# Seven half products for eight in the large products of a transformer block

## The chip, the cores and the metric

The kernel runs on one core of one Trainium2 chip. The metric is the time of one launch on the device in microseconds (us), as the median of several runs. The core has a matrix engine (TensorE, PE in the profile), two engines for element-wise work (VectorE, DVE; GpSimd, POOL), one for activations (ScalarE, ACT) and one that issues transfers (SyncE, SP). Each has its own instruction stream and executes it in the order in which it is written. Matrix products land in PSUM, which PE, DVE and ACT reach; POOL works in SBUF alone.

## The reference

One block over 2048 latent tokens of 1024 channels, with 256 context tokens, all in float32:

```python
q, k, v, p, gt = split(modulate(x, sh1, sc1) @ w_in)         # 1024 | 256 | 256 | 512 | 2048 columns
attn_o = banded_attention(rope(q), rope(k), v, k_c, v_c, sink)  # +-128 tokens and all context keys
attn_d = attn_o @ w_attn_branch                              # 1024 x 1024
pool_d = (multiscale_pool(p) per group @ w_pool) * pool_scale
merged = sigmoid(gt[:, :1024]) * attn_d + sigmoid(gt[:, 1024:]) * pool_d
x = layernorm(ALPHA * x + g1 * (merged @ w_out), ln1_g, ln1_b)
u = layernorm(x) * (1 + sc2) + sh2
h = square(relu(u @ w_mlp_in))                               # 1024 x 4096
x = layernorm(ALPHA * x + g2 * (h @ w_mlp_out), ln2_g, ln2_b)   # 4096 x 1024
```

The modulation (sh, sc, g) is one vector for all tokens, a product of silu(c) with w_ada.

## The kernel before, in words

Every large product is made of float32r matmuls of a high and a low part. `split` (L52 to L57) casts an operand to its high part on ACT (L54) and subtracts to get the low part on DVE, or on POOL where that is asked for (L57). `mm3` (L59 to L63) makes three matmuls of a pair: high with high, high with low, low with high.

The first phase (up to L647) makes the projections to q, k, v and the attention, block by block of 128 tokens; it leaves the modulated, transposed input in `u_scr` and the attention output in `a_scr`, both in DRAM. Its last blocks run beside the channels of two pooling groups (`early_pool`, L572). The order of PE is written out there (`PLAN`, manual_schedule).

The second phase (from L649) runs over two chunks of 1024 tokens (L716). In each chunk all stages follow one another with their intermediate values in SBUF: pooling channels (`p_group`, `p_finish`), pooling gates and pooled maps (`pool_gate`), attention gates, attention branch and merge, output projection (`out_mm`) with the first normalisation (`ln_affine`, `ln1_u`) and the transposed input of the MLP (`u2_half`), then the MLP by groups of 256 hidden channels (`mlp_in`, `mlp_out`) with the second normalisation (`ln2`). Weights come in tiles of 1 MB through two raw buffers (`raw_tile`), are scaled by a gate vector on POOL where needed (L661) and split into two pairs of buffers (`wtile`, `wcols`). Sixteen steps of column sums over w_ada (`ada_load`, `ada_sum`) lie between the stages of the first chunk. `chan_mm` (L672 to L680) makes products with channels on the partitions. Here a scheduler orders each engine's instructions at compile time, PE's too, by the order of the program and by what is ready.

Tiles with one tag share a number of buffers: a new tile waits until the last reader of the one whose place it takes is done.

## Time and profile before

| | |
|---|---|
| median of 3 runs | 3173.37 us (3172.95 to 3176.61) |
| span of the profiled execution, its own time from first to last instruction | 3174.3 us |
| PE, PE's weight loads | 98%, 82% of the span |
| DVE, POOL, ACT | 56%, 36%, 36% |
| mean granted clock of PE | 0.993 |
| moved by transfers | 207 MB, mean 65 GB/s |

The profile is one execution. A busy time is the union of an engine's instructions; matmul records are pipelined and overlap, so the rate of PE is read from start to start. The granted clock is 1.00 at 2.4 GHz and 0.50 at 1.2 GHz. "A <- B" beside an idle time means that B ended last before A could start.

### The profile page before, as it was taken

Reading aid. Unit: us, or ns where it says so; the run is one execution under the profiler, and the core shown is the slowest. Engines: PE = TensorE matmul, PEld = TensorE weight load, DVE = VectorE, ACT = ScalarE, POOL = GpSimd, SP = SyncE. Lnnn points to the kernel's source line nnn. Section 1 sums busy time; section 2 is a strip of 40 time slices with the busy share of each in tenths; the row PEclk is TensorE's granted clock in tenths of the full one; section 3 lists DMA queues with packets and bytes.
Section 4 is the critical chain, followed back from the end, with each engine's and each line's share of the span. In section 5 each row is a group of like instructions: output and inputs, shape, how many; then the busy total and the mean of one; then the engine's idle time right before and its main releaser. Section 6 shows DMA issues by size and latency. Waiting matters only on the chain.

```text
span 3174.3 us, 41663 instructions
## 1 busy us (share of the span) xinstructions
PE 3096.2 (98%) x16104; PEld 2616.7 (82%) x16104; DVE 1780.8 (56%) x3136; ACT 1128.2 (36%) x1985; POOL 1151.8 (36%) x1419
## 2 busy tenths in 40 slices
PE   8899999998999999899999999999999999999998
PEld 5799899997988889788888888788898788888886
DVE  5678788887774446644444455821448444444446
ACT  4577777777621222521112112311214311121111
POOL 2877777776420052422122221410234321222123
PEclk9999999999999999999999999999999999999999
DMA  7111111113154430211111112411321111111111
GB/s 244 35 30 41 35 31 41 35 31 105 28 160 128 146 107 28 67 41 53 53 41 54 40 53 66 142 52 40 107 93 54 40 53 44 50 53 41 53 40 53
DMA packets 157846, 207.04 MB, mean 65 GB/s; under 512 B 7248, under 2 KB 132304, under 8 KB 157648
## 3 DMA queue, kind: packets, MB, share of 16 engines
q1 hardware_dynamic: 157648, 204.38, 20.5%
q8 instruction: 127, 2.08, 0.3%
q14 instruction: 71, 0.58, 0.1%
HBM read 179.19 MB, written 25.17 MB: 64 GB/s over the span
## 4 chain that ended last, share of the span: by engine, by line
PE 87%; DVE 7%; DMA 2%; issue 2%; POOL 1%; ACT 1%; SPq 0%; DVEq 0%; POOLq 0%; ACTq 0%
PE ps_y L62 7%; PE ps_y L63 7%; PE ps_y L61 7%; PE ps_h L677 7%; PE ps_h L680 7%; PE ps_h L678 7%; PE ps_o L497 4%; PE ps_pt L480 4%; PE ps_s L444 3%; PE ps_ga L677 2%; PE ps_ga L680 2%; PE ps_ga L678 2%; PE ps_ab L677 2%; PE ps_ab L678 2%; PE ps_ab L680 2%; PE ps_s L445 2%
## 5 line engine op out<-in xcount | busy, mean ns | idle before, releaser
L57 POOL TENSOR_TENSOR ht<-r,ht 128x512 fp32r<-128x512 f32 x128 | 172.0, 1346 | 1009.0 <-ACT ht L54 946.3
L974 DVE TENSOR_TENSOR acc<-ps_y,acc 128x512 f32<-128x512 f32 x464 | 314.7, 689 | 366.6 <-PE ps_y L63 366.5
L54 ACT CAST wh<-raw 128x2048 fp32r<-128x2048 f32 (+1 forms) x102 | 189.1, 1857 | 828.9 <-PE ps_y L63 471.6
L678 PE MATMUL ps_h<-u,wh 128*128 128x512 f32 x1024 | 406.2, 397 | 10.3 <-DVE u L57 10.3
L62 PE MATMUL ps_y<-wl,ht 128*128 128x512 f32 x1024 | 405.0, 396 | 1.7 <-DVE wl L57 1.7
L680 PE MATMUL ps_h<-u,wl 128*128 128x512 f32 x1024 | 404.7, 396 | 0.0
L63 PE MATMUL ps_y<-wh,ht 128*128 128x512 f32 x1024 | 403.2, 394 | 0.0
L677 PE MATMUL ps_h<-u,wh 128*128 128x512 f32 x1024 | 401.3, 398 | 0.0
L61 PE MATMUL ps_y<-wh,ht 128*128 128x512 f32 x1024 | 400.6, 393 | 0.0
L57 DVE TENSOR_TENSOR wl<-raw,wh 128x2048 fp32r<-128x2048 f32 (+1 forms) x100 | 228.1, 2282 | 202.8 <-ACT wh L54 202.8
L951 DVE TENSOR_TENSOR r<-r 128x512 f32<-128x512 f32 x128 | 142.7, 1119 | 300.6 <-ACT r L950 300.6
L57 DVE TENSOR_TENSOR pl<-ps_pt,ph 128x512 fp32r<-128x512 f32 x312 | 212.6, 686 | 70.4 <-ACT ph L54 68.4
L678 PEld LDWEIGHTS ps_h<-u,wh 128*128 128x128 f32 x1024 | 193.2, 189 | 57.0 <-DVE u L57 12.1
L459 POOL TENSOR_SCALAR s<-s,sm 128x640 f32<-128x640 f32 (+1 forms) x256 | 202.3, 798 | 99.1 <-DVE sm L458 53.7
L456 ACT ACTIVATE s<-s,sm 128x641 f32<-128x641 f32 (+1 forms) x256 | 210.2, 822 | 66.6 <-DVE sm L450 66.1
L62 PEld LDWEIGHTS ps_y<-wl,ht 128*128 128x128 f32 x1024 | 192.1, 188 | 47.6 <-DVE wl L57 2.3
L61 PEld LDWEIGHTS ps_y<-wh,ht 128*128 128x128 f32 x1024 | 192.3, 188 | 46.9 <-ACT r L950 0.3
L680 PEld LDWEIGHTS ps_h<-u,wl 128*128 128x128 f32 x1024 | 193.5, 189 | 45.4
L677 PEld LDWEIGHTS ps_h<-u,wh 128*128 128x128 f32 x1024 | 193.2, 189 | 45.1
L450 DVE CUSTOM_DVE_ANT_0 s<-ps_s,mask,nsink 128x640 f32<-128x640 f32 (+1 forms) x256 | 211.4, 863 | 31.2 <-PE ps_s L445 30.6
L63 PEld LDWEIGHTS ps_y<-wh,ht 128*128 128x128 f32 x1024 | 192.2, 188 | 44.4
L54 ACT CAST ph<-ps_pt 128x512 fp32r<-128x512 f32 x312 | 179.7, 581 | 110.7 <-PE ps_pt L480 107.6
(217 smaller groups left out, 6931.2 us busy)
## 6 DMA issues: line engine op xcount, KB each, us to landing
raw<-w_mlp_in SPq DMA_DIRECT2D x32, 1024.0 KB, 5.5
raw<-w_mlp_out SPq DMA_DIRECT2D x32, 1024.0 KB, 4.8
raw<-w_in SPq DMA_DIRECT2D x19, 1024.0 KB, 5.5
raw<-w_ada SPq DMA_DIRECT2D x16, 1024.0 KB, 5.2
raw<-u_scr SPq DMA_DIRECT2D x8, 1032.0 KB, 5.4
adaw<-w_ada SPq DMA_DIRECT2D x16, 512.0 KB, 8.1
xt<-x SPq DMA_DIRECT2D x16, 512.0 KB, 3.6
u_scr<-u SPq DMA_DIRECT2D x32, 256.0 KB, 3.1
```

What stands on the lines that cost most here:

```text
L54: act.copy(hi, src)
L57: (lo_eng or dve).tensor_tensor(lo, src, hi.bitcast(F32), ALU.subtract)
L61: pe.matmul(ps, sh, mh, start=first, stop=False)
L62: pe.matmul(ps, sh, ml, start=False, stop=False)
L63: pe.matmul(ps, sl, mh, start=False, stop=last)
L450: dve.tensor_tensor_reduce(out=s[:, 0:n], in0=pieces[z][2], in1=mk[z], op0=ALU.add, op1=ALU.min, scale=-1.0 / math.sqrt(HD), scalar=nsink[ ...
L456: act.activation(s[:, 0:n + 1], s[:, 0:n + 1], AF.Exp, bias=sm[:, 0, j:j + 1], scale=-1.0, accum_out=sm[:, 1, j:j + 1])
L459: pool.tensor_scalar(s[:, 0:n], s[:, 0:n], sm[:, 2, j:j + 1], 1.0, ALU.mult, ALU.mult)
L677: pe.matmul(ps, wh[:, k, c:c + P], mh, start=k == 0, stop=False)
L678: pe.matmul(ps, wh[:, k, c:c + P], ml, start=False, stop=False)
L680: pe.matmul(ps, wl[:, k, c:c + P], mh, start=False, stop=k == KT - 1)
L974: dve.tensor_tensor(a, ps, a, ALU.add)
```

## The change

The first phase stays as it is. Behind it the pooling channels and pooled maps of both chunks are made first, and the maps go to DRAM (`pd_scr`). Then come, each over all tokens, the attention branch, both gates and the merge, the output projection with the first normalisation, the first MLP product, and the second one; their results go to DRAM between the stages (`ab_scr`, `mg_scr`, `x1_scr`, `u2_scr`, `h_scr`, the last 32 MB in size).

Every product of a stage is cut into items: a contraction over 1024, with 1024 x 1024 values of one operand that are fixed for a stage (`Fill`: 1024 tokens, or 1024 rows of w_out or w_mlp_out) and 1024 x 256 values of the other that are streamed (`Stream`: 256 weight columns, or 256 tokens). Both are cut in two along both dimensions, and the four blocks of the result come from seven products of blocks in Winograd's form of Strassen's scheme: the sums of blocks are made in float32 ahead of the split into two parts (`Combos`), three products start a PSUM bank (numbers 1, 6, 5) and four are added into one of these banks after DVE or ACT has read it (2, 7, 4, 3).

There are 96 items: 8 of the attention branch, 16 of the gates, 8 of the output projection, 32 of each MLP product. The fixed operand changes 10 times. An item's 7 products have 4 x 3 matmuls of 128x128 with 512 columns each. The whole second phase now has PE's order written out (`ms2`); the other engines are still ordered by the scheduler.

```diff
+    ms2.enter_context(tc.manual_schedule(engines={mybir.EngineType.PE}))
+    def rtile(...):  tag="R", bufs=8        # parts of the streamed operand
+    def etile(...):  tag="ext", bufs=2      # two of the sums; also the copy xn and the pooled maps
+    def rwtile(...): tag="rw", bufs=3       # raw fixed operand; the fourth tile is a raw_tile (2, with the streams)
+    def ltile(p): 8 slots for products 1, 2; 8 for 6, 7; 12 for 5, 4, 3   # four per product
+    class Combos:
+        def add(self, eng=None):
...
+                e.tensor_tensor(v[0], b12, b11, sub)
+                e.tensor_tensor(v[1], b22, v[0], sub)
+                e.tensor_tensor(b12, b22, b12, sub)
+        def late(self, eng=None):
+            e.tensor_tensor(b11, b12 if self.kind == "A" else b21, self.v[1], ALU.subtract)
...
+    class Stream:                            # Combos on POOL
+        def step(self, p):
+            t = rtile([P, 2, 4, P])
+            split(t[:, 0], t[:, 1], self.c.src(p))
+            self.t[p] = t
+            if p == 1:
+                self.c.late()
...
+    class Fill:
+        def load(self):
+            for j in range(4):
+                raw = rwtile([P, 2, 2, 512]) if j < 3 else raw_tile([P, 2, 2, 512])
+                sp.dma_start(raw.rearrange("p k h n -> p k (h n)"), self.src(j))
+                if self.scale is not None:
...
+                        (pool if j % 2 else dve).tensor_tensor(v, v, g, ALU.mult)
...
+            for j in (0, 1):
+                self.c[j].add()
+        def step(self, p):
+            every = range(4)
+            if p == 1:
+                self.split(1, every)
+                self.c[0].late()
+                self.c[1].late()
+            elif p in (6, 7):
+                self.split(p, (0, 1))
+            elif p in (2, 4):
+                self.split(p, every)
+            elif p == 5:
+                self.split(5, (0, 1))
+                for j in (2, 3):
+                    self.c[j].add(dve)
+                    self.c[j].late(dve)
+                for q in (6, 7, 5):
+                    self.split(q, (2, 3))
+            else:
+                self.split(3, every)
+    def prod(ps, p, R, L, first):
+        r = R.t[p]
+        for k in range(4):
+            m = L.t[p, k]
+            mm = ((r[:, 0, k], m[:, 0]), (r[:, 0, k], m[:, 1]), (r[:, 1, k], m[:, 0]))
+            for i, (a, b) in enumerate(mm):
+                pe.matmul(ps, a, b, ...)
+    def run_items(items):                    # the loop's body, for item it with the next one nxt
+            if n + 2 < len(items):
+                items[n + 2].stream.load()
+            nfill = nxt.stage if nxt and nxt.stage is not it.stage else None
+            if nfill:
+                nfill.load()
...
+            if nxt:
+                nxt.stream.c.add()
+            def after(p):
+                if nfill:
+                    nfill.step(p)
+                if nxt:
+                    nxt.stream.step(p)
+            X = ps2("ps_x")
+            prod(X, 1, R, L, True)
+            x = sttile("cx")
+            act.copy(x, X)
+            it.sink("x", x)
+            after(1)
+            Y = ps2("ps_y")
+            prod(Y, 6, R, L, True)
+            u2_ = sttile("cu")
+            dve.tensor_tensor(u2_, Y, x, ALU.add)
+            it.sink("u2", u2_)
+            after(6)
+            prod(X, 2, R, L, False)
+            it.sink(11, X)
+            after(2)
+            prod(Y, 7, R, L, False)
+            u3_ = sttile("cv")
+            dve.tensor_tensor(u3_, Y, x, ALU.add)
+            it.sink("u3", u3_)
+            after(7)
+            Z = ps2("ps_z")
+            prod(Z, 5, R, L, True)
+            it.sink(22, u3_, Z)
+            after(5)
...
+            prod(Y, 4, R, L, False)
+            it.sink(21, x, Y)
+            after(4)
+            prod(Z, 3, R, L, False)
+            it.sink(12, u2_, Z)
+            after(3)
...
+    def acc_sink(i, scaled, last):           # output projection and second MLP product
+        def begin():
+            for b in range(2):
+                a = ldp[0].tile([P, D], F32, name="acc", tag="acc", bufs=2)
...
+                sp.dma_start(a, (x if last == "ln1" else x1_scr)[rows, :])
+                if scaled:
+                    act.mul(a, a, ALPHA)
...
+        def sink(key, t, z=None):
+            if key == "x":
+                pool.tensor_tensor(at(21), at(21), t, ALU.add)
...
+            else:
+                dve.tensor_tensor(at(key), t if key == 11 else z, at(key), ALU.add)
+                if key in (21, 12):
+                    ... last_of(...)         # normalise where it is the last sum, then store
+    def h_sink(c, n):                        # first MLP product
...
+                dve.tensor_tensor(o, z, t, ALU.add)
+                dve.scalar_tensor_tensor(o, o, 0.0, o, op0=ALU.max, op1=ALU.mult)
+            sp.dma_start(h_scr[:, 2 * n + h, t0:t0 + 512], o)
```

The sinks of the gates load the pooled map or the branch, apply the sigmoid on ACT, multiply on DVE, and for the pooling gate add the stored other half on POOL; each block of 128x512 is stored. Twelve steps of the column sums over w_ada now lie at the starts of items of the branch and the gates (four and eight items), four in the first MLP product. In the output projection each of the two token blocks of an item is normalised, stored, normalised a second time (`xn`), transposed on PE in the next item and stored modulated.

## Rows read from the trace of the kernel before

**Rows 1.** The page's first part: busy time, share of the span, instructions.

```profile
PE 3096.2 (98%) x16104; PEld 2616.7 (82%) x16104; DVE 1780.8 (56%) x3136; ACT 1128.2 (36%) x1985; POOL 1151.8 (36%) x1419
```

**Rows 2.** Timeline of PE in three stretches: start us, length us, instruction.

```profile
1601.10 0.40 PE L62 MATMUL ps_y<-wl,ht 128*128 128x512 f32 x1
...
1611.79 0.39 PE L63 MATMUL ps_y<-wh,ht 128*128 128x512 f32 x1
...
2400.55 0.29 PE L61 MATMUL ps_out<-wh,mg 128*128 128x256 f32 x1
...
2401.97 0.28 PE L61 MATMUL ps_out<-wh,mg 128*128 128x256 f32 x1
...
880.61 0.32 PE L677 MATMUL ps_p<-uh,wh 128*128 128x344 f32 x1
...
889.11 0.32 PE L677 MATMUL ps_p<-uh,wh 128*128 128x344 f32 x1
```

**Rows 3.** Tile ps_p: count, ns min/median/max, first to last start.

```profile
L677 PE MATMUL ps_p<-uh,wh x144: 313/320/422, 866.7 to 2105.9; 128*128 128x344 f32 x144
```

**Rows 4.** Timeline at the end of the launch.

```profile
3159.58 0.39 PE L63 MATMUL ps_y<-wh,ht 128*128 128x512 f32 x1
...
3170.50 0.99 SPq L995 DMA_DIRECT2D out<-acc  x2
```

**Rows 5.** Waits of PE behind the attention: us in total, times, longest.

```profile
PE ps_pd L61 <- ACT poh L54: 7.0, 1, 7.0
```

**Rows 6.** Tiles r, acc and raw, columns as in rows 3.

```profile
L951 DVE TENSOR_TENSOR r<-r x128: 679/693/3984, 1302.8 to 3119.3; 128x512 f32<-128x512 f32 x128
L54 ACT CAST ht<-r x128: 619/622/640, 1303.5 to 3120.0; 128x512 fp32r<-128x512 f32 x128
L57 POOL TENSOR_TENSOR ht<-r,ht x128: 1264/1293/3221, 1304.2 to 3120.7; 128x512 fp32r<-128x512 f32 x128
...
L974 DVE TENSOR_TENSOR acc<-ps_y,acc x464: 642/692/697, 1379.7 to 3164.6; 128x512 f32<-128x512 f32 x155
...
L698 DVE SCALAR_TENSOR_TENSOR adacc<-raw,cs,adacc x94: 475/485/2023, 899.9 to 1061.0; 128x256 f32<-128x256 f32 x94
L661 POOL TENSOR_TENSOR raw<-raw,gb x40: 4599/4628/6725, 1120.6 to 3080.1; 128x2048 f32<-128x2048 f32 x40
```

**Rows 7.** Timeline of DVE and POOL in two stretches.

```profile
1277.05 2.28 DVE L57 TENSOR_TENSOR wl<-raw,wh 128x2048 fp32r<-128x2048 f32 x1
1279.24 4.58 DVE L92 SCALAR_TENSOR_TENSOR mv<-mv 128x1 f32<-128x1 f32 x1
...
1277.15 6.65 POOL L661 TENSOR_TENSOR raw<-raw,gb 128x2048 f32<-128x2048 f32 x1 [2.10 <-DMA raw<-w_mlp_out]
...
2497.51 3.66 DVE L972 SCALAR_TENSOR_TENSOR acc<-acc,ps_y 128x512 f32<-128x512 f32 x6
...
2498.71 4.62 POOL L661 TENSOR_TENSOR raw<-raw,gb 128x2048 f32<-128x2048 f32 x1
```

**Rows 8.** Timeline of PE behind a wait, and stretches: us, busy (count), clock, DMA share, GB/s.

```profile
1275.92 1.22 PE L678 MATMUL ps_h<-u,wh 128*128 128x512 f32 x2 [4.78 <-DVE u L57]
...
1276.00:1278.00 2.00, 2.00 (x5) 1.63 (x6) 2.00 (x4) 2.00 (x5) 0.85 (x1) 0.50 0.22 88
1278.00:1280.00 2.00, 2.00 (x8) 1.60 (x8) 2.00 (x2) 0.53 (x2) 2.00 (x1) 0.76 0.00 0
```

**Rows 9.** Tile acc in the normalisations, columns as in rows 3.

```profile
L897 DVE SCALAR_TENSOR_TENSOR acc<-acc,mv,lnp x23: 737/757/2424, 1997.9 to 3160.5; 128x512 f32<-128x512 f32 x23
...
L898 POOL TENSOR_TENSOR acc<-acc,lnp x23: 1264/1303/3080, 2015.0 to 3165.0; 128x512 f32<-128x512 f32 x23
```

**Rows 10.** DMA issues: count, KB each, median us to landing.

```profile
raw<-w_mlp_out SPq DMA_DIRECT2D x32, 1024.0 KB, 4.8
...
acc<-x SPq DMA_DIRECT2D x16, 512.0 KB, 4.8
out<-acc SPq DMA_DIRECT2D x15, 512.0 KB, 2.6
```

More of the change, by code (lines that the diff above doesn't have):

```diff
@@ new lines, in prod, with __init__ @@
+    def prod(ps, p, R, L, first):
[4 more added lines that the diff above has]
+            for i, (a, b) in enumerate(mm):
+                pe.matmul(ps, a, b, start=first and k == 0 and i == 0, stop=k == 3 and i == 2, skip_group_check=not first)
+    class Item:
+        def __init__(self, stage, stream, sink, begin=None):
+            self.stage, self.stream, self.sink, self.begin = stage, stream, sink, begin
@@ L683, in block_kernel @@
-    ones = lp.tile([P, P], F32, name="ones")
+            uh, ul = uu[k]
+            for i, ps in enumerate(pss_):
+                pe.matmul(ps, wh[:, k], uh[:, UP[i]:UP[i] + 344], start=k == 0, stop=False)
+                pe.matmul(ps, wh[:, k], ul[:, UP[i]:UP[i] + 344], start=False, stop=False)
+            for i, ps in enumerate(pss_):
+                pe.matmul(ps, wl[:, k], uh[:, UP[i]:UP[i] + 344], start=False, stop=k == KT - 1)
+        pt = ptp.tile([P, PW], F32, name="pt1", tag="pt1", bufs=2)
@@ L684, in block_kernel, with w_fill, row, bias_row @@
+    def w_fill(src, scale=None):
+        v = src.rearrange("(k j p) n -> p j k n", k=2, j=4)
+        return Fill("B", lambda j: v[:, j], scale)
+    def row(name):
+        return stp.tile([P, D], F32, name=name, tag="row", bufs=2)
+    def bias_row(name, c0):
+        r = row(name)
+        sp.dma_start(r, b_row[c0:c0 + D].partition_broadcast(P))
+        return r
+    ones = stp.tile([P, P], F32, name="ones")
     dve.memset(ones, 1.0)
-    gb = [lp.tile([P, D], F32, name=f"gb{i}") for i in range(2)]
```

657 lines of the change are left out of this document (351 added, 306 removed).

## The prediction

> **What bounds the kernel now.** I read the page's engine table first: TensorE (PE) is busy 98% of the span [rows 1]. Matmul records overlap, so I counted starts. Beside each other, 128x512 matmuls of the MLP start 0.2324 us apart (1601.10 to 1611.79, 46 intervals), the 256-column ones of the output projection 0.118 us (2400.55 to 2401.97, 12 intervals), the 344-column ones of the pooling channels 0.157 us (880.61 to 889.11, 54 intervals) [rows 2]. The phase behind the attention starts on PE at 866.7 [rows 3] and its last matmul starts at 3159.58; the launch ends 14.7 us after that [rows 4]. Its matmuls are 8448 of 512 columns (MLP 6144, gates 1536, attention branch 768), 1536 of 256, 432 of 344 and 96 for the pooled maps: 1963 + 181 + 68 + 22 = 2234 us, with about 20 us of transposes and column sums (estimate, from their counts). From 866.7 that ends at 3121; the real end leaves some 39 us for all waits of PE, the longest one 7.0 us [rows 5]. So this phase is matmul-bound nearly everywhere, and fewer matmuls are time, if the other engines keep up.
>
> **What is removed.** Each large product becomes 96 items of 7 x 4 x 3 = 84 matmuls of 512 columns: 8064 x 0.2324 = 1874 us for the 2144 before, 270 us less; one item is 19.5 us. Pooling's 90 us and the 20 us stay. The floor is 866.7 + 1874 + 90 + 20 + 14.7 = 2865 us, on the profiled execution's 3174.3, which is 0.9 us above the runs' median, so I add nothing for that. Everything below is what hinders this floor.
>
> **What is added on the other engines.** The parts are split after the sums, so per item seven 128x512 parts of the streamed operand are cast on ACT (0.62 us each, 4.3 in all: no bound) and subtracted on DVE (0.69 us, D), and POOL makes four sums (1.29 us, G) [rows 6]. The question is whether D and G add up. The timeline says they do: at 1277.15 a POOL product that usually takes 4.63 us took 6.65, behind a 2.28 us DVE subtraction, and a DVE operation on one column then took 4.58 us, until POOL was done. DVE additions that read PSUM ran six in 3.66 us beside such a POOL product [rows 7]. The median and the maximum agree: 0.693 and 3.98 us with both inputs in SBUF, 0.692 and 0.697 us with one in PSUM [rows 6]. So I count D and G as one serial resource, "the port", and operations with a PSUM input outside it.
>
> The Trainium skill, "SBUF — State Buffer", "Who interferes with whom", states the same lock and that the loser waits for the whole instruction. Against a heavy price stands the median of that product with both inputs in SBUF, which is its undisturbed time: in this trace the two seldom meet. With no lock at all a hand-over below would cost 9 us, with the lock 17; I take the lock.
>
> Port time of an item: stream 7D + 4G = 10.0 us. The attention branch adds none; MLP in adds G + 3D: 13.4; MLP out adds 3G: 13.9; gates 4D, and 4G in each second item: 12.8 and 17.9, with 3.7 us of modulation sums (7 x 0.485 plus one) in eight of them, where a pair then averages 19.1 [rows 6]. All fit into 19.5 on average. With a normalisation it is more: per token block two POOL and two DVE operations (1.30 and 0.76 us [rows 9]) and small ones, about 4.1 us. MLP out with LN2: 13.9 + 8.2 + 1 = 23.1. The output projection has 3G, two blocks and a second statistic: 24.1.
>
> **Stalls, item by item.**
> - *Hand-overs, 10 of them.* The fixed operand's 28 parts fill exactly the 28 slots, so part p of the next stage can be written only after the last item's product p and is needed one item later: between the end of product 1 and the start of the next item's last product lie 33.5 us. Into them must go 28D for the parts, 8D of sums on DVE, 2G, twelve D and four G of the next stream, and some 5.8 us of sinks: 51.9 us less what can be put off. Lower bound 9 us over (the stream after next is postponed), upper 29 (nothing overlaps, and the fourth raw tile, which shares two buffers with the streams, comes a 4.8 us transfer late [rows 10]). I take 17, nearer the lower end because the order written down gives the fill precedence. Five of the hand-overs also scale their tile: 4 x 1.4 + 4 x 2.3 = 14.8 us of port, at best hidden in earlier items (0), at worst all of it; I take 4. Sum 170 + 20 = 190, bounds 90 to 364. These holes also cost clock: behind a wait of 4.78 us the granted clock was 0.50, the 1.2 GHz level, for two us and 0.76 on average for the next two [rows 8]. That is inside the 17.
> - *First fill and end of pooling.* The last pooled map (a chain of about 15 us) and the first 28 parts follow each other; PE order is fixed by hand there. 30 us (15 to 38), and 10 (0 to 25) for pooling's own chains; the 7.0 us wait of before [rows 5] is one of these.
> - *Output projection with LN1, 8 items.* Port alone 24.1 - 19.5 = 4.6 us over. There are also only two accumulator tiles: add, statistics and affine about 8 us, second statistics and copy about 5, reload 4.8, scaling and one POOL addition 2.6: 21 us from one use to the next. With DVE's PSUM reads and eight statistics counted as D each not hidden at all it is 33.7. I take 26.4: 55 us, bounds 37 to 114.
> - *MLP out with LN2, 8 items.* 3.6 to 10.5 us over; I take 4.4: 35 (29 to 84).
> - *Gates.* DVE's five PSUM reads (3.4 us) come to the 19.1: 0 to 3 us in eight items, so 0 to 24; I take 12.
> - *Accumulators elsewhere.* Store 2.6 and load 4.8 us [rows 10] end about 9 us into the next item; the PSUM bank waiting is used again two items later. Nothing; if that cover went, one product's wait, counted in the next point.
> - *In every item* PE waits twice for DVE to read a bank before it adds to it, with one product (2.8 us) between. DVE is in order, and one POOL operation in front of it eats 1.3 us of that. 0 to 1.3 us per item, I take 0.5: 45 us (0 to 125).
> - *SP's queue* gains stores and reloads: at most 5 MB in an item of gates. 1 MB lands in 4.8 us [rows 10], so that could fill it; I charge nothing beyond the upper bounds, since loads are two items ahead.
>
> Sum: 2865 + 190 + 30 + 10 + 55 + 35 + 12 + 45 = **3242 us**, taken as 3240, 2% slower. With all lower ends 3036, with all upper ends 3639.
>
> **Rivals.**
> - *Faster: the port is not felt.* POOL's sums fall where DVE reads PSUM or waits, and the order chosen for POOL, DVE and SP reaches ahead (loads, scaling and the first sums of a fill in the items before). Then DVE alone sets the hand-over: 36D + 12D + about 9 us of sinks is 42 in 33.5 us, 9 over, ten times 90; LN stages cost their lower ends 66, the start 25, handshakes 15: 2865 + 196 = 3061 us. For it: port use is below 14 of 19.5 us in 64 of 96 items, and the attention ran with long DVE and POOL times and few PE waits [rows 1, 5]. Against it: the 4.58 us row [rows 7], and that a fill is a dense run of just the operations that exclude each other. It decides once a hand-over costs under about 10 us. The Trainium skill, "Perfetto Trace Analysis", "Optimizing Scalar/DVE Operations", leans against this rival: moving work from DVE to GpSimd may not help, since they share a read port.
> - *Much slower: latency, not throughput.* Each sum waits in a chain (slot free, cast, subtract, two scratch tiles handed from the fill to the stream and back), engines execute in a fixed order, and PE at 1.2 GHz doubles each product that follows a hole. With hand-overs of 36 us, LN items of 33.7 and 1.3 us in each item: 2865 + 360 + 40 + 198 + 125 = 3588 us at its worst, about 3450 in the middle. For it: PE's two LN stretches show such chains already [rows 5, 8]; against: they lost only a few us there.
> - *The floor is reached.* All hidden but the start: about 2900 us. Against it: the LN stages exceed the item on the port alone.
> - *The change doesn't do what it says:* if sums were not fewer matmuls PE would stay at 3121 plus all stalls, near 3500. The count of 84 per item excludes it; I give it nothing.
>
> **How the numbers follow.** Forecast, 3180 to 3400: 0.48. Port not felt, 3000 to 3167: 0.31. Floor: 0.04. Much slower, over 3400: 0.13. Within 0.2% (6 us, about what a measurement can tell): 0.04. So faster 0.35, same 0.04, slower 0.61. The range takes the rival in, 3050 to 3450; the forecast's own is 3180 to 3400.
>
> **What would show it.** PE should hold 8064 + 528 large matmuls behind 866.7 at 0.232 us start to start inside an item, and items of 19.5 to 20.5 us in MLP in and out. Each change of the fixed operand should show a hole or a slow stretch of 15 to 25 us with DVE and POOL together near the whole window and DVE subtractions of 1.3 to 2 us; the LN items should take 24 to 28 us. The step on the port is wrong if DVE subtractions keep 0.69 us at the hand-overs; the step on hand-overs is wrong if PE's items there take under 29 us; the floor is wrong if plain items take over 21 us.

## The result, and the profile after

The changed kernel takes 3467.37 us (median of 4 runs, 3466.19 to 3470.29), beside 3174.85 us (3172.95 to 3176.61) for the kernel before: 1.092 times, 95% interval 1.091 to 1.094. Slower was forecast, but 3240 us; the time lies 17 us above the range of 3050 to 3450, and 67 us above the forecast's own, 3180 to 3400.

The page first. It gives each engine's busy time, and below that its busy tenths and TensorE's granted clock in 40 slices of the span; this is the changed kernel, to be held against [rows 1].

```profile
PE 2938.9 (85%) x14184; PEld 2432.6 (70%) x14184; DVE 2391.2 (69%) x3965; ACT 1556.1 (45%) x2867; POOL 1745.8 (50%) x1890
...
PE   8899999999858989797666599979996969789576
...
DVE  4687788877676787867555766685567575666775
...
PEclk9999999999879989898878799989997989899788
```

PE has fewer matmuls (14184, before 16104), but it is busy 85% of a longer span instead of 98%. Its row is full (9) only in stretches, and in every slice in which it falls to 7 or less the clock's row shows 8 or less. So the work went, as forecast, and more waiting came than work went.

To find the dents I use one regular mark of an item: ACT's copy of the first product (`cx`). ACT's timeline of the changed kernel (start, duration, engine, line, operation) around the change from the first to the second stage of the first MLP product:

```profile
2211.76 0.59 ACT L850 COPY cx<-ps_x 128x512 f32<-128x512 f32 x1 [2.17 <-PE ps_x L805]
...
2231.09 0.59 ACT L850 COPY cx<-ps_x 128x512 f32<-128x512 f32 x1 [2.17 <-PE ps_x L805]
...
2250.43 0.59 ACT L850 COPY cx<-ps_x 128x512 f32<-128x512 f32 x1
...
2291.64 0.57 ACT L850 COPY cx<-ps_x 128x512 f32<-128x512 f32 x1
...
2319.03 0.59 ACT L850 COPY cx<-ps_x 128x512 f32<-128x512 f32 x1 [2.13 <-PE ps_x L805]
```

Start to start, a plain item takes 19.3 us. The last item of a stage takes 41.2 here and the next stage's first one 27.4. Below, the price of a hand-over is what these two take above 2 x 19.3: here 30.0 us. The windows of the same kernel (busy times, then granted clock, DMA share, GB/s) show a plain stretch and this hand-over:

```profile
2020.00:2194.00 174.00, 174.00 (x757) 141.86 (x756) 110.71 (x163) 47.26 (x80) 61.69 (x45) 1.00 0.39 126
...
2250.40:2319.00 68.60, 45.03 (x169) 35.00 (x169) 59.80 (x69) 24.07 (x43) 31.07 (x18) 0.80 0.37 128
```

In the plain stretch PE never stops, at 174.00 / 757 = 0.230 us for a matmul, where the forecast took 0.2324 [rows 2]. In the hand-over DVE is busy 59.8 of 68.6 us, and PE, at a mean clock of 0.80, takes 45.03 / 169 = 0.266 us for each. The same windows over all ten hand-overs give 279 us of idle PE and 466 us of busy PE, where twenty items of 19.3 us are 386. So some 80 of the 359 us that they cost are not waits but slower matmuls around the waits, at mean granted clocks of 0.75 to 0.84 (a few of the 80 are transposes).

With all 96 marks the time adds up: the first product of the items starts at 994.7 instead of 956.7 (866.7 + 90); 96 items at 19.3; what they take beyond that; and the end of the launch as forecast. LN1 and LN2 are the two normalising stages, the output projection and the last MLP output stage; plain items are the 62 outside of these, the hand-overs and both ends.

| us above the floor | forecast | measured |
|---|---|---|
| start of the items | 10 | 38 |
| first item | 30 | 35 |
| ten hand-overs, with scaling | 190 | 359 |
| output projection with LN1 | 55, and a part of the floor's 20 for transposes and column sums | 130 in its six middle items (the rest is in two hand-overs) |
| last MLP stage with LN2 | 35 | 62 in six middle items |
| gates, handshakes in every item | 12 + 45 | 16 in 62 plain items |
| item of 84 matmuls | 19.5 | 19.3: 19 us less in all |

PE's waits behind 860 us, in the changed kernel (who waits for what: total, times, longest):

```profile
PE ps_x L805 <- ACT La L57: 151.7, 10, 17.9
PE ps_z L805 <- DVE acc L1110: 107.1, 21, 10.1
PE ps_u L1144 <- ACT xn L1138: 55.8, 6, 11.8
PE ps_y L805 <- DVE Lb L60: 41.5, 11, 5.1
```

The first row has one wait for each of the ten hand-overs (the first product needs a part of the fixed operand's fourth tile, which comes last); the second and the third lie mostly in the normalising stages. Before, PE's longest wait behind the attention was 7.0 us [rows 5]. The dearest hand-over is the one out of the output projection, 60.7 us; the other nine cost 23 to 45.

Who is slow in the hand-over is in DVE's groups of 2250.4 to 2319.0 by form (busy us, mean ns of one, then idle time before them):

```profile
L60 DVE TENSOR_TENSOR R<-raw,R 128x512 fp32r<-128x512 f32 x10 | 11.5, 1170 | 0.7 <-ACT R L57 0.7
L763 DVE TENSOR_TENSOR rw<-rw,gb 128x1024 f32<-128x1024 f32 x4 | 7.7, 1975 | 0.0
...
L60 DVE TENSOR_TENSOR Lc<-rw,Lc 128x512 fp32r<-128x512 f32 x6 | 3.8, 681 | 0.0
...
L1170 DVE SCALAR_TENSOR_TENSOR cv<-cv 128x512 f32<-128x512 f32 x2 | 3.6, 1778 | 0.0
```

Undisturbed, 512 columns take 0.68 us (third row), as [rows 6] said; beside POOL the same operations take 1.2 to 1.8. All of this trace behind 1000 us says so too. Of DVE's two-input operations (TENSOR_TENSOR) on 512 columns, 662 had both inputs in SBUF and no POOL operation beside them for over 0.1 us: at most 0.70 us each. 459 had both in SBUF and POOL beside them: 1.26 us on average, up to 2.88. 215 had an input in PSUM and POOL beside them: at most 0.69. And L763, which isn't this stage's, stands here: it scales the weights of the stage after, whose buffers have just come free.

### The profile page after: what moved, and what is told of

The parts are those of the page before. It is cut to its first block, busy times and chain, and to the rows that moved or that the text cites. A ratio compares the mean times of both kernels' runs of the same rounds, so it can differ in the third digit from the quotient of the medians.

```text
span 3464.2 us, 42248 instructions
## 1 busy us (share of the span) xinstructions
PE 2938.9 (85%) x14184; PEld 2432.6 (70%) x14184; DVE 2391.2 (69%) x3965; ACT 1556.1 (45%) x2867; POOL 1745.8 (50%) x1890
## 5 line engine op out<-in xcount | busy, mean ns | idle before, releaser
L805 PE MATMUL ps_x<-La,R 128*128 128x512 f32 x2304 | 601.5, 410 | 173.4 <-ACT La L57 151.7
L805 PE MATMUL ps_z<-Lc,R 128*128 128x512 f32 x2304 | 589.6, 407 | 107.2 <-DVE acc L1110 107.1
L805 PE MATMUL ps_y<-Lb,R 128*128 128x512 f32 x2304 | 596.0, 407 | 87.9 <-DVE Lb L60 41.5
L805 PEld LDWEIGHTS ps_x<-La,R 128*128 128x128 f32 x2304 | 452.0, 197 | 289.5 <-ACT La L57 156.1
L805 PEld LDWEIGHTS ps_z<-Lc,R 128*128 128x128 f32 x2304 | 452.5, 198 | 217.0 <-DVE acc L1110 98.3
L57 ACT CAST R<-raw 128x512 fp32r<-128x512 f32 (+1 forms) x486 | 301.1, 626 | 660.0 <-PE ps_z L805 310.0
L805 PEld LDWEIGHTS ps_y<-Lb,R 128*128 128x128 f32 x2304 | 447.2, 195 | 209.0 <-DVE Lb L60 45.9
L60 DVE TENSOR_TENSOR R<-raw,R 128x512 fp32r<-128x512 f32 (+1 forms) x486 | 452.0, 934 | 109.3 <-ACT R L57 107.2
L805 PE MATMUL ps_y<-Lc,R 128*128 128x512 f32 x1152 | 294.2, 406 | 6.6 <-DVE cv L864 6.4
L805 PEld LDWEIGHTS ps_y<-Lc,R 128*128 128x128 f32 x1152 | 224.6, 197 | 56.4 <-DVE cv L864 8.8
L453 DVE CUSTOM_DVE_ANT_0 s<-ps_s,mask,nsink 128x640 f32<-128x640 f32 (+1 forms) x256 | 211.3, 862 | 29.6 <-PE ps_s L448 29.4
```

The source lines that it names most:

```text
L57: act.copy(hi, src)
L60: (lo_eng or dve).tensor_tensor(lo, src, hi.bitcast(F32), ALU.subtract)
L453: dve.tensor_tensor_reduce(out=s[:, 0:n], in0=pieces[z][2], in1=mk[z], op0=ALU.add, op1=ALU.min, scale=-1.0 / math.sqrt(HD), scalar=nsink[ ...
L805: pe.matmul(ps, a, b, start=first and k == 0 and i == 0, stop=k == 3 and i == 2, skip_group_check=not first)
```

## The experiments

I call **excess** what DVE's operations of 512 and 1024 columns take above 0.68 and 1.36 us each, added up from the by-form groups of the two items of all ten hand-overs. It measures how long DVE stood behind POOL: 141 us in the changed kernel. (Undisturbed, 1024 columns take 1.21 us, so the sum is some 3 us too small where there are 20 of them.) The letters L, P, Q and so on are the theories that each expectation names. A time without a range is that of one run. Edits are to the changed kernel unless a base is named. Base "swap and table" is e1 with e2; it did not run by itself, and its 3368 us and hand-over sum of about 307 are added up from the two.

**e1: the late fourth tile.** Its buffer is shared with the streams, whose load was issued first.

```diff
-            if n + 2 < len(items):
-                items[n + 2].stream.load()
             nfill = nxt.stage if nxt and nxt.stage is not it.stage else None
             if nfill:
                 nfill.load()
+            if n + 2 < len(items):
+                items[n + 2].stream.load()
```

> The changed kernel with one edit: at a hand-over the next fixed operand is loaded before the stream tile of the item after next, so its fourth raw tile takes the raw buffer that is free at the start of the last item and not the one that the next item's splits hold until its end. Theory L (the hand-over is a latency: the fourth raw tile lands late and its seven parts hold PE): the hole of some 15 us before the first product of a new stage goes, the ten hand-overs fall from 338 us over the plain items to about 170, total near 3300 us. Theory P (the hand-over is the throughput of DVE and POOL on their shared port): the same work has to be done, the hand-overs stay at 300 to 340 us, total 3430 to 3470 us.

3403.5 us, hand-over sum 312: the tile was late, but this is worth 46 us in the hand-overs, not the 168 of theory L. Theory P had the sum right and the time too long. In the hand-over shown above 30.0 turned only into 29.1. The 15 us hole ahead of the first product went, and other waits took its place (PE, 2224.6 to 2292.3):

```profile
PE ps_y L805 <- ACT Lb L57: 8.3, 1, 8.3
PE ps_y L805 <- DVE cv L864: 6.9, 1, 6.9
PE ps_y L805 <- DVE cu L856: 2.9, 2, 2.1
```

DVE's timeline in e1 says why `cv` comes late:

```profile
2265.88 0.68 DVE L856 TENSOR_TENSOR cu<-ps_y,cx 128x512 f32<-128x512 f32 x1
2266.48 1.15 DVE L60 TENSOR_TENSOR R<-raw,R 128x512 fp32r<-128x512 f32 x1
2267.56 6.74 DVE L763 TENSOR_TENSOR rw<-rw,gb 128x1024 f32<-128x1024 f32 x2
2274.22 1.52 DVE L60 TENSOR_TENSOR R<-raw,R 128x512 fp32r<-128x512 f32 x1
2275.67 4.48 DVE L763 TENSOR_TENSOR rw<-rw,gb 128x1024 f32<-128x1024 f32 x2
```

Between `cu` and `cv`, both of which PE waits for, the next stage's scaling holds DVE for over 11 us; four such operations undisturbed are 4.8 (1.21 each).

**e2: activation tables.** In the output projection ACT's timeline of the changed kernel shows loads of tables inside each normalisation:

```profile
1718.49 0.29 ACT L92 ACTIVATE mv<-mv,eps 128x1 f32<-128x1 f32 x1 [1.92 <-DVE mv L91]
1718.80 1.28 ACT L93 ACT_TABLE_LOAD   x1
1720.10 0.20 ACT L93 ACTIVATE mv<-mv 128x1 f32<-128x1 f32 x1
1720.32 1.28 ACT L92 ACT_TABLE_LOAD   x1
1721.61 0.30 ACT L92 ACTIVATE mv<-mv,eps 128x1 f32<-128x1 f32 x1
```

In the two normalising stages there are 43 at L92 and 43 at L93, 110 us of ACT; the kernel before has 5 loads in all. The set that holds both functions is asked for at 1584.64, but two sigmoids of the last gate come behind it, with a load of their own at 1586.57. The edit asks for it when they are over.

```profile
1584.64 1.28 ACT L1193 ACT_TABLE_LOAD   x1
...
1586.57 1.28 ACT L1075 ACT_TABLE_LOAD   x1
```

```diff
-                tc.keep_in_program_order(act.preload_act_table_set(EXP_LN))     # in ln1_begin
...
         if what == "ln1":
+            if b == 1:
+                tc.keep_in_program_order(act.preload_act_table_set(EXP_LN))
             ln_affine(t, *lnr["ln1"])
```

> The changed kernel with one edit: the load of the activation table that holds both the logarithm and the exponential is placed at the first normalisation of the output projection, behind the last sigmoid, instead of at the start of that stage. Theory: the 86 table loads of 1.28 us lie in the normalisation's chain of waits, so the items of the output projection fall from about 40 to 34 us and those of the last MLP stage from 30 to 26, total near 3390 us. Rival: ACT has room beside the chain, the items stay within 1 us, total 3440 to 3470 us.

3431.7 us: 36 us less, 23 of them in LN1's six middle items (130 to 107), with 3 loads in all. Items of the output projection fell from 40.9 to 37.1 us, not to 34, and those of the last MLP stage hardly: between theory and rival. The Trainium skill, "ScalarE: Activation LUTs", "What ACT_TABLE_LOAD costs", has 1283 ns for a load, as the trace has, and a drain of 1380 ns with it; here the next operation starts 0.02 us behind the load, so no such drain shows, and the measurement decides.

**e3, e4: no block sums on POOL**, with the old order of loads and with the swap.

```diff
     def add(self, eng=None):          # and late() likewise
         e = eng or self.eng
+        if e is pool:
+            ... return                # the products read raw blocks
```

> The changed kernel without the sums of blocks on POOL (those of the streams and of two of the four tiles of each fixed operand are left out, their products read raw blocks; DVE's sums stay). Theory P: DVE alone has 42 us of work in the 33.5 us window, so a hand-over falls from 34 to about 10 us over, total near 3220 us. Theory L: the fourth raw tile still comes only when the next stream's splits are done, some 5 us earlier than before, so the ten hand-overs fall by 50 to 80 us, total 3370 to 3410 us.

> Both edits of e1_swap and e3_nopool. Theory P: like e3_nopool, near 3220 us, and e1_swap adds nothing. Theory L with a port share below it: the late tile and then the port are taken away, hand-overs of 5 to 10 us over the plain items, total near 3200 us, while e1_swap alone is near 3300 and e3_nopool alone near 3390 us.

3302.6 and 3279.2 us; hand-over sums 242 and 215; first item 30 instead of 54 us. From e1 to e4 the hand-overs lose 98 us and DVE's excess falls from 151 to 53, by 98: in sum, POOL's sums cost what DVE stands behind them. Hand-over by hand-over it does not come out so: the one out of the output projection loses 3 us for 7 of excess, the one into the second MLP input stage 20 for 9. Three hand-overs with little excess left (into the attention branch's second half, the first gates and the second MLP input stage: 0, 0 and 3.5) cost 7.4, 10.8 and 8.8 us. DVE is busy for 87 to 94% of them, so I read this as DVE's own time. The other seven still cost 17 to 54 us, so neither theory's 3200 to 3220 us came.

**e5: the fill's sums of tiles 0 and 1 on DVE** (base swap and table, 3368 us by addition).

```diff
             for j in (0, 1):
-                self.c[j].add()
+                self.c[j].add(dve)
...
-                self.c[0].late()
-                self.c[1].late()
+                self.c[0].late(dve)
+                self.c[1].late(dve)
```

> The changed kernel with the next stage's fill issued ahead of the stream (the swap), the activation table loaded in front of the first layer norm, and the eight block sums of tiles 0 and 1 of each fill moved from POOL to DVE; the stream's sums stay on POOL. Base by addition of the two single runs: 3403.5 - (3467.4 - 3431.7) = 3368 us, hand-over sum 312. Theory P (DVE and POOL share one resource, and an operation of two inputs from SBUF holds it for 0.69 us on DVE and 1.29 us on POOL): each of 10 fills gives back 8 x 0.6 = 4.8 us of the resource and the DVE operations that stood behind POOL's; hand-over sum 230 to 265, first item 5 to 10 us shorter, 3300 to 3325 us. Theory Q (DVE's own queue is full in a hand-over and its order decides): DVE gets 8 x 0.69 = 5.5 us more in each fill, hand-over sum 312 to 365, 3368 to 3425 us.

3378.9 us, hand-over sum 296. A miss for P (230 to 265): of the 48 us of shared time that it should give back some 10 to 16 arrive (excess 132). Q had the time, but not the sum (312 or more). That DVE's longer queue took the rest is likely, not shown.

**e6: weights loaded and scaled in the middle of the stage before** (base swap and table).

```diff
+    def early(self, j, ins):                       # of a weight fill
+        with tc.issue_after(ins):                  # behind the stream's load of this item
+            self.load((j,), False)                 # load and scale tile j, no sums yet
...
+            for j in range(3):                     # in run_items: tile j, 4 - j items ahead
+                m = n + 4 - j
+                if ...: items[m].stage.early(j, items[n + 1].stream.ins.ins)
```

> Swap and table as above (base 3368 us), and tiles 0 to 2 of the weights for the output projection and the four MLP output stages are loaded, and scaled where they are scaled, in three items in the middle of the stage before instead of in its first item. Theory S (the scaling of the next stage's weights sits in the first item of a stage, in front of the eviction operations that PE waits for): the five hand-overs with such scaling in their first item (into the second gate stage, into the second MLP input stage, into MLP output stages 0 to 2) get 8 to 15 us shorter each, so the hand-over sum falls from 312 to 240 to 270 and the time to 3300 to 3330 us. Rival M (the work has to be done somewhere, and DVE and POOL have no room in a plain item): the middle items that take a scaled tile grow from 19.3 to 22 or more, time 3355 to 3385 us. Rival 0 (the scaling waits are only what is left when the sums are late): hand-over sum within 15 of 312, 3353 to 3383 us.

3334.4 us. The time is 4 us above S's range. S was right about the place: hand-over sum 248, and the hand-overs into the second MLP input stage and into MLP output stages 0 to 2 fell from 29, 34, 35, 34 (e1) to 18, 20, 21, 21. M was right about the items, not about the time: middle items of the MLP output stages went to 20 to 27 us, 62 plain items took 20.03 on average instead of 19.52, 32 us together. In those items PE now waits for DVE (e6, 2571 to 2690):

```profile
PE ps_z L812 <- DVE acc L1121: 8.2, 4, 3.6
PE ps_y L812 <- DVE cv L875: 3.9, 1, 3.9
```

**e7: longer chains of accumulators** (base swap and table): those of every second item, and the normalised rows `xn`, in the idle fill buffers; PE's transposes behind product 3.

```diff
-                a = ldp[0].tile([P, D], F32, name="acc", tag="acc", bufs=2)
+                if i % 2 and (last == "ln2" or last and i < 7):
+                    if not b:
+                        pair = rwtile([P, 2, D], "acc")
+                    a = pair[:, b]
+                else:
+                    a = ldp[0].tile([P, D], F32, name="acc", tag="acc", bufs=2)
...
-            for f in todo:                         # behind product 5, ahead of 4
-                f()
...                                                # now behind product 3; xn likewise in an rwtile
```

> Swap and table as above (base 3368 us; LN1, the six middle items of the output projection, some 97 to 105 us over 6 x 19.3; LN2, those of the last MLP output stage, some 55 over). In both normalising stages the accumulators of every second item lie in an idle fill buffer, so that those of the next item can be loaded while a normalisation still runs; in the output projection the normalised rows lie there too, no longer in the buffers of the stream's sums, and PE turns them after product 3 instead of before product 4. Theory A (a chain through two accumulator buffers: normalise, store, load, scale, then the next product's eviction): LN1 falls to 20 to 50 us over, LN2 to 5 to 25 over; 3260 to 3300 us. Rival N (DVE, POOL and their shared resource are simply full of the normalisation's own operations): LN1 stays at 85 or more, LN2 at 45 or more; 3345 to 3375 us.

3326.2 us: LN1 70, LN2 22 above plain items. A holds for LN2; LN1 lies between A (20 to 50) and N (85 or more), and the time 26 us above A's range. PE's waits in the output projection's middle items, first of the changed kernel (1633.2 to 1878.5):

```profile
PE ps_u L1144 <- ACT xn L1138: 40.2, 4, 11.8
PE ps_z L805 <- DVE acc L1110: 32.8, 6, 7.1
PE ps_u L1144 <- ACT u2f L1148: 13.9, 4, 6.7
```

and of e7 (1628.7 to 1814.2):

```profile
PE ps_u L1159 <- ACT u2f L1163: 16.1, 12, 3.5
PE ps_z L805 <- DVE acc L1115: 14.5, 2, 9.3
PE ps_z L805 <- DVE mv L96: 5.3, 1, 5.3
```

The wait for `xn` is gone. Items with odd numbers (counted from 0) still take 37 to 42 us, the even ones 22 to 23. In the odd ones of the middle PE is idle for 10 to 15 us, half or more of it in one wait for DVE (5 to 9 us, ahead of a product into `ps_z`), and busy for 6 to 10 us longer than in the even ones, at granted clocks of 0.83 to 0.86. What keeps DVE there isn't settled.

**e8: e5, e6 and e7 together.**

> All of it together: swap, table, fill sums on DVE, the weights' loads and scaling in the middle of the stage before, and the longer chains of accumulators in the two normalising stages. If the three theories P, S and A hold and add up: 3368 - 55 - 55 - 90 = 3170 us (3130 to 3210), level with the kernel before. If the rivals Q, M and N hold: 3360 us or more. A time between, 3210 to 3360, is read by the sums of the hand-overs and of the two normalising stages.

3286.3 us: hand-overs 240, LN1 72, LN2 22, plain items 20.29. From the single runs 3303 was to be expected (3368 + 11 - 34 - 42), so the edits add up to within 17 us, but to nothing near the 3170 of theories P, S and A. What e6 and e7 cost in plain items stays (in e7 and e8 the modulation sums' matmuls had moved behind product 3 as well).

**e9: no fills** (base swap and table).

```diff
             if nfill:
-                nfill.load()
+                nfill.t, nfill = it.stage.t, None
```

> Swap and table (base 3368 us, hand-over sum about 300). From the second stage on nothing is filled: each stage uses the parts of the first fixed operand again, so the loads, sums, parts and scaling of ten fills are left out (the values are wrong, the matmuls the same in number and shape). It weighs the fills as a whole. If all of what the ten hand-overs lose is the fill's work on DVE, POOL and ACT and the clock behind its holes, the hand-over sum falls to 20 to 50 (the start and end of the normalising stage remain) and the scaling's cost elsewhere goes too: 3060 to 3110 us, below the kernel before. If a change of stage loses time without a fill (the reordering of accumulators, scratch through DRAM), the sum stays above 80 and the time above 3140.

3085.7 us; the hand-overs cost 24.1 in sum, 20.2 of them at the end of the first normalising stage. Elsewhere a change of stage by itself costs nothing; filling does, some 280 us of the 3368.

**e10 and e17: the exclusion, or the wait for the cast?** Both leave the subtraction of the cast part out in the fills and keep DVE's count and sizes. e10 gives DVE one input in PSUM; e17 gives it the same block twice, both inputs in SBUF. Neither waits for ACT's cast (base swap and table).

```diff
-                split(t[:, 0], t[:, 1], self.c[j].src(p))
+                act.copy(t[:, 0], self.c[j].src(p))
+                dve.tensor_tensor(t[:, 1], self.c[j].src(p), zero_ps, ALU.subtract)             # e10
+                dve.tensor_tensor(t[:, 1], self.c[j].src(p), self.c[j].src(p), ALU.subtract)    # e17
```

> Swap and table (base 3368 us, hand-over sum about 300 to 312). In the fills alone, DVE's second part is made from the block and a bank of zeros in PSUM, not from the block and its cast in SBUF: the same count of DVE operations of the same size, but none that takes both inputs from SBUF (this leaves out the subtraction of the cast part, and with it the wait for the cast). Theory P (the resource that DVE and POOL share makes the hand-over): the 28 operations of a fill no longer stand behind POOL's sums, nor POOL's behind them; hand-over sum 190 to 240, and DVE's fill operations stay at 0.69 us in the hand-overs. Theory Q (DVE's own time and the order of its queue make it): 28 x 0.69 us stay on DVE; hand-over sum 270 to 312. With one bank fewer for the transposes the output projection may be up to 15 us slower; it is left out of the reading.

> e10 with the exclusion put back: in the fills DVE's second part is made from the block twice (block minus block, both inputs in SBUF), so it doesn't wait for ACT's cast, as in e10, but DVE and POOL exclude each other, as in the changed kernel. The subtraction of the cast part is left out. Swap, table and one bank fewer for transposes as in e10 (3312 us, hand-over sum 234.5; with the true subtraction 3368 and 300 to 312). Theory P (exclusion): hand-over sum 280 to 312, 3350 to 3380 us. Theory W (the wait for the cast, a chain over two engines): hand-over sum 225 to 255, 3300 to 3330 us. Between them, 255 to 280, each has its share.

e10: 3312.0 us, hand-over sum 234.5, excess 70. e17: 3395.0 us, hand-over sum 319.6, excess 146. So W falls: with the exclusion, and without the wait, the whole cost is back, 85 us in the hand-overs and 76 in the excess, even somewhat more than P had (280 to 312). DVE's groups in the hand-over into MLP output stage 1, of e10 (2692.5 to 2756.7):

```profile
L60 DVE TENSOR_TENSOR R<-raw,R 128x512 fp32r<-128x512 f32 x10 | 10.6, 1071 | 0.0
...
L777 DVE TENSOR_TENSOR La<-rw,zero_ps 128x512 fp32r<-128x512 f32 x4 | 2.6, 681 | 0.0
L777 DVE TENSOR_TENSOR Lc<-ext,zero_ps 128x512 fp32r<-128x512 f32 x4 | 2.6, 682 | 0.0
L777 DVE TENSOR_TENSOR Lb<-rw,zero_ps 128x512 fp32r<-128x512 f32 x3 | 2.0, 682 | 0.0
```

and of e17 (2750.1 to 2823.5):

```profile
L60 DVE TENSOR_TENSOR R<-raw,R 128x512 fp32r<-128x512 f32 x10 | 12.5, 1258 | 0.0
...
L777 DVE TENSOR_TENSOR Lb<-rw 128x512 fp32r<-128x512 f32 x3 | 5.8, 1946 | 0.0
L777 DVE TENSOR_TENSOR La<-rw 128x512 fp32r<-128x512 f32 x5 | 5.4, 1121 | 0.0
L777 DVE TENSOR_TENSOR Lc<-ext 128x512 fp32r<-128x512 f32 x4 | 4.8, 1227 | 0.0
```

With an input in PSUM all take 0.68 us beside a busy POOL; with two in SBUF up to 1.95. One reserve: the scheduler orders DVE by its own costs, so the order differs in places. In the hand-over into the second MLP input stage (13.0 in e10, 27.9 in e17) at least 27 of the 29 fill operations take 0.68 us in each, and e17 has both pairs of scaling in front of `cv` where e10 has one. So the split between exclusion and order is only as good as the sums: hand-over sum less excess is 161 (e1), 162 (e4), 164 (e10), 173 (e17). Where something else is longer, the excess is no price: with the late tile this difference is 218 (changed kernel), with e13's longer chain below 198.

**e11, e12, e18: what helped, together.** e11 is e1, e2, e6 and e7 with the modulation sums' matmuls at their old place and the scaling in 512 columns, all on DVE; e12 has e5 as well; e18 is e12 again.

```diff
                     for k in range(2):
-                        v = raw[:, k].rearrange("p h n -> p (h n)")
-                        (pool if j % 2 else dve).tensor_tensor(v, v, g, ALU.mult)
+                        for h in range(2):
+                            v = raw[:, k, h]
+                            dve.tensor_tensor(v, v, g[:, 512 * h:512 * h + 512], ALU.mult)
```

> What helped, together: swap, table, weights of the five scaled or plain weight fills loaded in the middle of the stage before, the accumulators and normalised rows of the two normalising stages in idle fill buffers, PE's transposes behind product 3 but the modulation sums ahead of product 4 as they were, and the scaling in operations of 512 columns, all on DVE. Against the 3286 us of the earlier sum of edits: the modulation sums back at their place -15, scaling that holds the shared resource for 0.69 instead of up to 5 us at a time -20 to -40, POOL's sums back on POOL 0 to +15. 3235 us (3215 to 3275): still above the kernel before. If the scaling's mere amount is what the middle items pay (theory M), 3265 to 3290.

> The same with the fill's eight sums of tiles 0 and 1 on DVE. Alone they gave 16 us in the hand-overs and lost it in other items. Theory Q (DVE's queue): 0 to 20 us slower than with POOL's sums. Theory P: 10 to 40 us faster.

> The kernel of e12 again, for an interval: 3270 to 3285 us, a ratio to the kernel before of 1.030 to 1.035.

e11: 3296.5 us (4 runs, 1.038 times before, interval 1.036 to 1.040), not 3235, and above theory M's 3265 to 3290 too: hand-overs 251, plain items 20.10. No gain of the short scaling shows: e12 differs from e8 by it and by the old place of the modulation sums and is 10 us faster, less than the 15 that were expected of the place alone. e12: 3276.7, 20 us faster, as P said; e18: 3271.6 us (3267.6 to 3274.2), 1.031 times before (1.030 to 1.033), the fastest that leaves nothing out, and still 98 us slower than before.

**e13 to e16: the exclusion avoided with the true values**, by a copy of the cast in PSUM. e13 is e12 with it in the fills; e14 is e11 with it in fills and, outside hand-overs, streams; e15 is e14 without the early weights; e16 is e14 with the fill's sums on DVE.

```diff
+    def split_ps(hi, lo, src):
+        act.copy(hi, src)
+        z = ps2("ps_s", "s", 2)                    # the products keep 4 banks
...
+        act.copy(z, hi.bitcast(F32))
+        dve.tensor_tensor(lo, src, z, ALU.subtract)
```

> The best sum of edits so far (3277 us, hand-over sum 234) with the fills' parts made another way, and the same values: ACT casts the block into SBUF as before and copies the cast to one of two PSUM banks, and DVE subtracts that copy, so its operation has one input in PSUM. 28 x 0.62 = 17.4 us more on ACT in each hand-over (ACT was busy 25.9 of 69 us there), DVE's count unchanged; the products have four banks instead of six. Theory P (exclusion of DVE and POOL): with the fill's sums already on DVE the streams' sums and the MLP's additions are what POOL still has, so part of e10's 70 us is left to win: hand-over sum 170 to 205, 3215 to 3255 us. Rival C (the chain cast, copy, subtract through two banks is longer than the subtraction it relieves) or Q (DVE's own time): hand-over sum 230 or more, 3270 to 3330.

> As the last, but with all block sums on POOL, and the streams' parts made by way of PSUM too, outside of the hand-overs. Theory P: in middle items nothing of DVE's stream work excludes POOL any more (7 x 0.69 us less of the shared resource), so the items that scale a tile come back from 20 to 26 us towards 19.3 (some 40 us in all), and the hand-overs lie at 150 to 200 in sum: 3170 to 3230 us. Rival C: ACT has 7 x 0.62 us more in each item and its chain holds up PE's evictions on ACT; middle items above 20 us, 3290 or more.

> As e14 but with the weights' loads and scaling where the scheduler puts them, in the first item of the stage before. Theory P: plain items at 19.3, the five hand-overs that scale stay 8 to 12 us longer than the others; within 25 us of e14 on either side. If the scaling in middle items costs nothing once the exclusion is gone, e14 is 30 to 50 us faster than this.

> As e14 with the fill's sums of tiles 0 and 1 on DVE. Theory P: with the parts off the shared resource POOL has room for its sums, and DVE's queue is the fuller one; 0 to 30 us slower than e14. Theory Q and C: equal within 10.

3338.8, 3313.7, 3306.5 and 3320.4 us: P's sums and times are missed in e13 and e14, and C's come (e13 is 9 us above its range); e15 and e16 lie 7 us from e14 and decide nothing. DVE's excess falls to 59 (e13) and 58 (e14), but the hand-overs cost 257 and 258 (e12 234, e11 251), and the first item takes 64 us instead of 49 to 55. From e12 to e13 ACT's busy time in the hand-overs grows from 275 to 409 us and PE's waits there for ACT from 67 to 84, while those for DVE stay at 104. The products also have four PSUM banks instead of six; what that costs by itself was not tried. PE's waits of e14 (1000 to 3320):

```profile
PE ps_y L821 <- ACT R L57: 61.3, 11, 18.7
PE ps_y L821 <- ACT Lb L687: 40.6, 11, 5.7
PE ps_z L821 <- DVE acc L1139: 37.0, 15, 10.6
```

## Why the prediction was right in direction and wrong in size

- **The floor held.** Fewer matmuls at 0.230 us, plain items at 19.3 us, the end of the launch as forecast; e9, without fills, goes below the kernel before.
- **"Hand-overs, 10 of them ... I take 17", and 4 more for scaling in five of them: the failing step.** 190 was forecast, 359 measured: 36 us each where 17, and 4 more for scaling in five, were taken. That is just inside the term's own upper bound of 364; the choice near the lower end, "because the order written down gives the fill precedence", is what failed. The mechanism (DVE and POOL as one serial resource, a window that is too short) is the one the runs show, and two of its sizes were about right. DVE alone was put at 9 us in the rival; e4 shows 7.4 to 10.8 where nothing else disturbs. The exclusion was put at 8 us each, 80 in all; the edits that take a part of it away gave 85 (e10 against e17) and 98 (e1 against e4). Three terms were mis-sized or missing:
  - Scaling was put at 20 and "at best hidden in earlier items". The scheduler hoisted it into the first item of the stage before, ahead of operations that PE waits for; four hand-overs there fell from 132 to 79 us together when it left (e6), and 32 us of that came back in items that had no room.
  - The late fourth tile was only in the upper bound, as a transfer of 4.8 us; the hole was 15 us, and the tile is worth 46 in all (e1).
  - The hand-over out of the output projection was priced like the others; it takes 60.7 us, and 20.2 without any fill (e9). What makes the rest of it is open.

  The slower matmuls around the holes were seen, but put "inside the 17"; some 80 of the 359 us are theirs. These figures overlap, so they don't add up to 359. The forecast's list of a hand-over's work is also added up wrongly: its terms give 46.7 us, not 51.9. The 17 was chosen between the bounds and doesn't follow from either.
- **"Output projection with LN1 ... I take 26.4" for an item: 40.9 measured in the middle ones.** The chain through two accumulators was seen and priced too low (e7 takes off 27 to 37 us, from the 97 to 107 with e2's edit). Two things were not seen: the tables (23 us, e2), and the normalised rows, which lie in the two buffers that the sums also need and for which PE's transposes wait (55.8 us of waits). LN2 was 62 instead of 35 for the same chain; e7 brings it to 22.
- **"PE waits twice for DVE ... 45" and gates 12: too dear.** 16 us in 62 plain items. DVE is busy 64% of a plain stretch, and the waits found room. These 41 us too many hid a part of the miss.
- **Pooling's end, 10: 38.** Two waits for the first part of a pooled map are 11.6 us of it; the rest is open.
- **The rivals.** "Much slower", with a chance of 0.13, came nearest, and not only by its number: at its worst it had 360 us for the hand-overs and 198 for the normalising items, and 359 and 191 were measured; only its 125 for a wait in every item was far off. Its mechanism, latency, holds in part. It is what the normalising stages show, and in the hand-overs the late tile (46 us) and the slower matmuls behind holes (some 80) are of its kind. But it has no place for the exclusion: taking the wait for the cast away gave nothing (e17), taking the exclusion of the fill's own parts away gave 85. "The port is not felt" would have needed hand-overs under 10 us, which happens only where POOL's sums are gone. Of the signs named, DVE subtractions of 1.3 to 2 us at the hand-overs were there; items of 24 to 28 us in the normalising stages were not (29.6 and 40.9 on average).

## What to carry to other kernels

A scheme that trades matmuls for additions has to be priced where its additions bunch: not by an item's mean load (here PE is nearly full in 62 of 96 items), but by the window between the last use of an operand's parts and the first use of the next ones, with every other job that the freed buffers set off in the same window. When two engines exclude each other, moving operations between them gave little here (10 to 16 us in the hand-overs in e5, 20 in all in e12), and a detour over a third engine lost more than it saved (e13); what won was less work (e4, e9) and work at another time, less what it costs there (e6). A wait of the matrix engine should be priced above its length: of 359 us in the hand-overs some 80 were slower matmuls. And each stage that a reordering puts in a new neighbourhood needs its state checked: table sets, shared buffers, the place of loads in a queue.

## What was not expected of the hardware

- DVE's operations with one input in PSUM keep 0.68 us beside POOL, also when they write SBUF and read their other input there (e10: 0.681 and 0.682 us on average, in a window in which POOL was busy for 41.9 of 64.2 us). The Trainium skill, "SBUF — State Buffer", "Who interferes with whom", says the same of instructions with one SBUF input; the trace agrees.
- POOL loses time as well, and not only one operation's worth. In e1's hand-over into the second MLP input stage its sums of blocks take 1.3 to 2.3 us, where 1.3 is undisturbed, but the one that starts at 2256.58 takes 6.22: DVE ran nine two-input operations in a row, the last one ending at 2261.67, each in 0.68 us, and POOL was done 1.1 us after it. Three more of e1's sums on POOL stand like this beside a row of such operations (5.84, 5.32 and 4.64 us).
- DVE's rate is not its record's length: in that row the operations start 0.60 us apart (2257.37 to 2260.99) and last 0.68 each.
- Two functions of 0.29 and 0.20 us on one column, each with its own table load, cost 2.6 us of loads a pair (1.28 each).
